# S5 in a two-layer diffusion trunk: elementwise work on VectorE alone, with both directions in scan order

## The chip, the cores and the metric

The kernel runs on one core of one Trainium2 chip. A core has TensorE (PE in the profile) for matmuls, VectorE (DVE), ScalarE (ACT) and GpSimd (POOL) for elementwise work, SyncE (SP), which issues DMAs here, and 16 DMA engines. Each engine takes its instructions in the order of its own queue; an instruction whose operands are not ready holds up all that is queued behind it. The metric is the time of one execution on the device in microseconds. The median of three runs of the kernel before is 2175.32 us (2174.04 to 2178.39).

## What is computed

The reference is a trunk of two layers. In each, a modulated RMSNorm feeds one input projection and three token mixers side by side: an S5 state-space model, a bidirectional Mamba-2 (SSD) and windowed attention. Their outputs are merged through gates; then a second norm feeds an expert-choice mixture of 16 SwiGLU experts. There are 256 latent and 256 context tokens of width 1024. The change touches S5 only: 32 groups of 16 channels, each with 64 complex states, run once forward and once backward.

```python
def s5_scan(u, abr, abi, bbr, bbi, h0, reverse):
    if reverse:
        u = jnp.flip(u, 1)
    bur = jnp.einsum('gpk,bngk->bngp', bbr, u)
    bui = jnp.einsum('gpk,bngk->bngp', bbi, u)
    ...   # h[n] = a * h[n-1] + bu[n], complex, over the tokens

def s5_readout(hr, hi, c_re, c_im, reverse):
    y = (jnp.einsum('gkp,bngp->bngk', c_re.astype(F32), hr)
         - jnp.einsum('gkp,bngp->bngk', c_im.astype(F32), hi))
    return jnp.flip(y, 1) if reverse else y
```

The backward direction scans the context tokens in reverse and then the latent tokens in reverse. In layer 1 only latent tokens are needed at the output.

## The kernel before

The program runs mixing of layer 0 (0 to about 702 us), its experts (to 1188), mixing of layer 1 (to about 1680) and its experts (to the end). S5 is a generator, `s5_gen`, of eight batches a layer, four groups in each. The host function of the mixing calls one batch at four places in the SSD loop and one after each of four pairs of attention heads; the input projection (L122, L125, from split weights of L113) and the modulation matmuls (L165) fill TensorE in between. A scheduler that follows a model of times turns the program into one order for each engine; the pools of tiles set which instruction must wait for which.

Within a batch the 512 tokens are 64 chunks of 8. Steps and lines:

1. DMAs of ScalarE's queue load `bc` (B and C) and `Ub` (the input by chunk).
2. `bb`, the discretised B, three rows on VectorE and three on GpSimd (L614 to L619); ScalarE puts them into `bst` (L620, L621).
3. For each direction d, d = 0 on VectorE and d = 1 on GpSimd: `gp`, the input block of a chunk (L631 to L633, with `tmp`), and `cp9`, the output table (L637 to L639). `gp` is transposed on TensorE (L642) and evicted to `ti` by ScalarE (L643).
4. `pk` (L648): the in-chunk kernel. ScalarE and VectorE copy it into `kr` (L650 to L653), a part of the tile of `tmp`; a DMA stores it to `kd` in DRAM (L655) and four DMAs read it back as the Toeplitz tile `W` (L657).
5. The rotation table `er`, `ei` (L665 to L667, the real half on VectorE, the other on GpSimd).
6. `px` (L674): the input of every chunk. Eight products with the rotation on VectorE (L683 to L686), read from PSUM, two sums on GpSimd (L687, L688), eight scans of 64 columns on VectorE (L691), products for the rotation back (L696 to L699) and the shifted states `hs` (L706 to L709) on both engines.
7. `yp`: per group one matmul with `W` (L713) and two with `cp9` and `hs` (L715); then the GELU on ScalarE and VectorE and a store.

All four PSUM results (two transposes, pk, px, yp) take their bank from the tag `s5`, which has one buffer, so they follow each other in the order in which the program asks for them. The SBUF tiles (four of 128 x 2048, named rb) hold one batch and are used again by the next: a write into `tmp` waits until the store of `kr` to `kd` has read it.

## Time and profile before

| | us |
|---|---|
| median of three runs | 2175.32 (2174.04 to 2178.39) |
| span of the profiled execution | 2175.6 |
| TensorE busy | 1879.4 (86%) |
| VectorE busy | 1040.2 (48%) |
| GpSimd busy | 589.0 (27%) |
| ScalarE busy | 554.9 (26%) |

The busy shares are means over stages with different limits. In the expert stages the DMA engines move some 409 GB/s and TensorE waits for weights. In the mixing stages TensorE is close to full, and the other engines prepare what it reads. What S5 is worth is therefore read from the mixing stages, from the waits of TensorE and the order in which instructions stand there.

### The profile page before, as it was taken

The numbers are of one execution on the slowest core, as the hardware profiler recorded it, in microseconds if no ns is written. First come the engines' busy times: TensorE is split into PE (matmuls) and PEld (weight loads), VectorE is DVE, ScalarE is ACT, GpSimd is POOL, SyncE is SP. The second block draws the span as 40 slices with busy tenths as digits, with TensorE's granted clock in tenths as the row PEclk, the third lists the DMA queues.
The fourth block names the chain that finished last, engine by engine and source line by source line (L and its number), as shares of the span: only waits on it lengthen the run. The fifth ranks groups of instructions, "written<-read, shape, count | busy, mean of one in ns | idle before, by whom it ended". The sixth has DMA issues, their size and how long they took to land. (4 is left out here: it accounts for less than half of the span.)

```text
span 2175.6 us, 29618 instructions
## 1 busy us (share of the span) xinstructions
PE 1879.4 (86%) x11292; PEld 1127.1 (52%) x11292; DVE 1040.2 (48%) x2234; ACT 554.9 (26%) x1200; POOL 589.0 (27%) x644
## 2 busy tenths in 40 slices
PE   6899999999999997986897898989998997776675
PEld 4577777788787432322332576778897322111111
DVE  6888786663256227121123469788656222212122
ACT  4335644442343100000000433535443100000000
POOL 1645476542242002000003235486533000000000
PEclk9999989999998998998898998989998899999798
DMA  9464333336345998999999355343477899999997
GB/s 268 156 183 127 114 90 107 99 104 220 90 155 203 410 349 351 409 408 409 404 409 351 107 185 172 107 129 86 125 244 271 348 409 409 409 409 409 409 409 274
DMA packets 265310, 561.72 MB, mean 258 GB/s; under 512 B 44048, under 2 KB 132560, under 8 KB 264912
## 3 DMA queue, kind: packets, MB, share of 16 engines
q1 hardware_dynamic: 232864, 541.83, 68.0%
q10 hardware_dynamic: 32304, 18.00, 3.0%
q8 instruction: 89, 1.46, 0.3%
q14 instruction: 53, 0.43, 0.1%
HBM read 552.00 MB, written 7.77 MB: 257 GB/s over the span
## 5 line engine op out<-in xcount | busy, mean ns | idle before, releaser
L122 PE MATMUL bk_mm<-hh,wh 128*128 128x512 f32 (+1 forms) x704 | 254.2, 375 | 12.5 <-ACT xp L800 6.7
L122 PE MATMUL bk_mm<-hl,wh 128*128 128x512 f32 (+1 forms) x704 | 247.6, 365 | 0.0
L113 POOL TENSOR_TENSOR wl<-w,wh 128x1024 fp32r<-128x1024 f32 x64 | 157.0, 2452 | 223.5 <-ACT wh L110 171.1
L110 ACT ACTIVATE wh<-w 128x1024 fp32r<-128x1024 f32 x140 | 147.9, 1058 | 215.9 <-PE bk_mm L122 106.6
L125 PE MATMUL bk_mm<-hh,wl 128*128 128x512 f32 (+1 forms) x704 | 163.0, 361 | 1.5 <-POOL wl L113 1.5
L122 PEld LDWEIGHTS bk_mm<-hh,wh 128*128 128x128 f32 x704 | 139.6, 199 | 36.1 <-ACT xp L800 8.2
L122 PEld LDWEIGHTS bk_mm<-hl,wh 128*128 128x128 f32 x704 | 139.6, 199 | 17.7 <-issue 1.4
L113 DVE TENSOR_TENSOR wl<-w,wh 128x1024 fp32r<-128x1024 f32 x76 | 99.8, 1315 | 72.6 <-ACT wh L110 32.4
L125 PEld LDWEIGHTS bk_mm<-hh,wl 128*128 128x128 f32 x704 | 119.6, 195 | 20.0 <-POOL wl L113 1.7
L1389 PE MATMUL bk_mm<-rb,xeT 128*64 128x512 f32 x512 | 122.1, 601 | 3.3 <-DMA rb<-w_e_up 2.0
L1419 PE MATMUL bk_mm<-xw,xeT 128*32 128x512 f32 x448 | 107.3, 628 | 16.5 <-DMA xw<-w_e_gate 11.4
L1424 DVE SCALAR_TENSOR_TENSOR hd<-fth,bk_mm 64x512 f32<-64x512 f32 x16 | 10.9, 681 | 208.4 <-ACT fth L1422 208.4
L1441 DVE SCALAR_TENSOR_TENSOR YE<-bk_mm,grow 32x512 f32<-32x512 f32 x64 | 44.0, 687 | 129.6 <-PE bk_mm L1436 115.8
L1422 ACT ACTIVATE fth<-bk_mm 64x512 f32<-64x512 f32 x16 | 9.4, 590 | 377.7 <-PE bk_mm L1419 377.7
L1389 PE MATMUL bk_mm<-xw,xeT 128*64 128x512 f32 x320 | 82.1, 613 | 13.5 <-DMA xw<-w_e_gate 13.5
L603 POOL MEMSET rb<- 128x256 f32 x2 | 1.2, 588 | 319.0 <-PE bk_mm L1389 305.0
L1393 DVE SCALAR_TENSOR_TENSOR fth<-fth,bk_mm 128x512 f32<-128x512 f32 x16 | 11.0, 687 | 157.3 <-ACT fth L1392 157.3
L1389 PEld LDWEIGHTS bk_mm<-rb,xeT 128*64 128x64 f32 x512 | 40.1, 139 | 78.6 <-issue 69.8
L1409 DVE SCALAR_TENSOR_TENSOR YE<-bk_mm,grow 32x512 f32<-32x512 f32 x64 | 44.0, 687 | 73.3 <-PE bk_mm L1405 56.5
L1419 PE MATMUL bk_mm<-rb,xeT 128*32 128x512 f32 x304 | 68.0, 603 | 8.3 <-DMA rb<-w_e_up 6.1
L1366 PE MATMUL bk_ps<-YE,Gt 128*128 128x512 f32 x128 | 61.7, 612 | 11.9 <-DVE YE L1441 9.1
L1419 PEld LDWEIGHTS bk_mm<-xw,xeT 128*32 128x32 f32 x448 | 24.1, 114 | 88.7 <-issue 55.5
(560 smaller groups left out, 3883.5 us busy)
## 6 DMA issues: line engine op xcount, KB each, us to landing
xw<-w_e_gate SPq DMA_DIRECT2D x67, 1024.0 KB, 11.5
rb<-w_e_up SPq DMA_DIRECT2D x59, 1024.0 KB, 17.4
xw<-w_e_down SPq DMA_DIRECT2D x54, 1024.0 KB, 14.0
w<-w_in SPq DMA_DIRECT2D x92, 512.0 KB, 4.7
rb<-w_e_gate SPq DMA_DIRECT2D x43, 1024.0 KB, 16.6
w<-w_mod SPq DMA_DIRECT2D x80, 512.0 KB, 4.1
xw<-w_e_up SPq DMA_DIRECT2D x29, 1024.0 KB, 14.0
w<-w_e_down SPq DMA_DIRECT2D x46, 512.0 KB, 14.0
```

Source lines behind the costliest of these rows:

```text
L110: S.activation(r(hi), raw, AF.Copy)
L113: e.tensor_tensor(r(lo), raw, hi, op=OP.subtract)
L122: PE.matmul(ps, wh(m, k), xv, start=first and k == 0 and i == 0, stop=False)
L125: PE.matmul(ps, wl(m, k), xs[k](m)[0], start=False, stop=last and k == n - 1)
L1366: PE.matmul(ps, Gt[:, tt - tts[0], e // ne, :], YE[:, tt // 2 if full else 0, n, :], start=True, stop=True)
L1389: PE.matmul(ps[64 * n:64 * n + 64, :], xeT[:, k, e, :], w[:, n * 512:n * 512 + 512], start=k == 0, stop=k == 7)
L1393: V.scalar_tensor_tensor(th, th, 1.0, pg, op0=OP.add, op1=OP.mult)
L1409: V.scalar_tensor_tensor(YE[q0:q0 + 32, si, n, :], py[o:o + 32, :], 0.5, g2[o:o + 32, si, n * 512:n * 512 + 512], op0=OP.mult, op1=OP.mult)
L1419: PE.matmul(pg[o:o + 32, :], xeT[:, k, e, :], w[:, n * 512:n * 512 + 512], start=k == 0, stop=k == 7)
L1422: S.activation(th[:64], pg[:64], AF.Tanh, scale=0.5)
L1424: V.scalar_tensor_tensor(hd[64:128], th[:64], 1.0, pg[:64], op0=OP.add, op1=OP.mult)
L1441: V.scalar_tensor_tensor(YE[q0:q0 + 32, 0, n, :], py[o:o + 32, :], 0.5, g2[o:o + 32, 1, n * 512:n * 512 + 512], op0=OP.mult, op1=OP.mult)
```

## The change

- All elementwise work of S5 stands on VectorE; GpSimd keeps three fills at the start of a layer.
- Both directions are kept in scan order. The direction d = 1 is mirrored by the matmuls of px and yp, which read `Ub` and `hs` with a negative step; the rotation needs no mirrored views.
- px is laid out by real and imaginary part first, so that one row of 512 columns turns both parts of all groups (L659), two rows of 256 make the sums (L660, L661), and one scan of 512 columns (L662) does all eight sequences. Its factor `rho` is written out to 512 columns with a zero at the start of each sequence, by two ScalarE copies (L614).
- The tables `Aa` and `Ab` have 9 columns in place of 10. `cp9` is made for all nine places in five rows (L665, L670, L671); the ScalarE copies into it (L626) are gone.
- px is asked for ahead of pk, so the `s5` bank goes transposes, px, pk, yp. `er`, `ei` (L654 to L656), the rotation (L659 to L661), the scan and `cp9` stand ahead of `pk` (L676), `kr` (L678 to L681), the store to `kd` (L683) and the loads of `W` (L685). The rotation back (L692, in layer 1 L696), `hs` (L701, L702) and `yp` (L706, L709) follow.

The diff, without most of the removed lines, which are printed above:

```diff
-        Aa = keep("aa", 640).rearrange("p (q i) -> p q i", i=10)
-        Ab = keep("ab", 640).rearrange("p (q i) -> p q i", i=10)
-        G.memset(Aa, 0.0)
-        G.memset(Ab, 0.0)
+        Aa = keep("aa", 576).rearrange("p (q i) -> p q i", i=9)
+        Ab = keep("ab", 576).rearrange("p (q i) -> p q i", i=9)
...
-                    ov = ov[:, :, :, 1:10] if d == 0 else ov[:, :, :, 0:9]
...
-            xr, xi = sl(4, 64), sl(4, 64)
+            rho = sl(8, 64)
-            kr = tmp.rearrange("p a b -> p (a b)")[:, 784:1024]
-            pq = ti.rearrange("p a b -> p (a b)").rearrange("p (i t c) -> p i t c", i=4, t=4)
+            flat = lambda v: v.rearrange("p a b -> p (a b)")
+            kr = flat(tmp)[:, 784:1024]
+            xx = flat(gp)[:, :512].rearrange("p (r t) -> p r t", r=2)
+            PQ = flat(ti).rearrange("p (i r t) -> p i r t", i=2, r=2)
+            mir = lambda v: v.rearrange("p (s c) -> p s c", s=2)[:, :, ::-1]
+            G.memset(rho, 0.0)
...
+                for ri in range(2):
+                    S.activation(rho[:, 4 * ri:4 * ri + 4, 1:64], sp["rho"][:, q4, None].to_broadcast([128, 4, 63]), AF.Copy)
+                ft = flat(tmp)
+                for i, nm in enumerate(("fr", "fi")):
+                    V.tensor_tensor(ft[:, 256 * i:256 * i + 256].rearrange("p (r t k) -> p r t k", r=2, k=16), bc[:, 0:2],
+                                    sp[nm][:, None, g8, None].to_broadcast([128, 2, 8, 16]), op=OP.mult)
+                fb = bb.rearrange("p r t k -> p r (t k)")
+                V.tensor_tensor(fb[:, 0], ft[:, 0:128], ft[:, 384:512], op=OP.subtract)
+                V.tensor_tensor(fb[:, 1], ft[:, 128:256], ft[:, 256:384], op=OP.add)
                 S.activation(bst[0:64, :, 0:16], bb[0:64, 0], AF.Copy)
...
                 for d in range(2):
+                    for dst, r_, tb in ((gp, 0, A_), (tmp, 1, B_)):
+                        V.tensor_tensor(dst[:, td].rearrange("p t (k s) -> p t k s", s=8),
+                                        bb[:, r_, td, :, None].to_broadcast(sh),
+                                        tb[:, td, None, d:d + 8].to_broadcast(sh), op=OP.mult)
+                V.tensor_tensor(flat(gp), flat(gp), flat(tmp), op=OP.add)
+                for d in range(2):
                     pt = bank("s5")
                     for j in range(4):
                         PE.transpose(pt[:, j * 128:j * 128 + 128], gp[:, 4 * d + j], ident)
+                    S.activation(ti[:, 4 * d:4 * d + 4].rearrange("p t n -> p (t n)"), pt, AF.Copy)
+                px = bank("s5")
+                pxv = px.rearrange("p (r t c) -> p r t c", r=2, t=4)
+                for d in range(2):
+                    for j in range(4):
+                        g2 = j % 2
+                        uv = Ub[:, j, :] if d == 0 else mir(Ub[:, j, :])
+                        for ri in range(2):
+                            o = pxv[64 * g2:64 * g2 + 64, ri, 2 * d + j // 2, :]
+                            PE.matmul(o if d == 0 else o.rearrange("p (s c) -> p s c", s=2),
+                                      ti[:, 4 * d + j, 64 * ri:64 * ri + 64], uv, start=True, stop=True)
...
+                for i, (dst, x0, x1, op) in enumerate(((er, "E8r", "E8i", OP.subtract), (ei, "E8i", "E8r", OP.add))):
+                    dv = dst.rearrange("p t (m i) -> p t m i", i=8)
+                    tv = xt[:, i].rearrange("p t (m i) -> p t m i", i=8)
+                    V.tensor_tensor(dv, E8[x0], F8["F8r"], op=OP.mult)
+                    V.tensor_tensor(tv, E8[x1], F8["F8i"], op=OP.mult)
+                    V.tensor_tensor(dv, dv, tv, op=op)
+                turn_ = [flat(v)[:, None, :].to_broadcast([128, 2, 256]) for v in (er, ei)]
+                for i in range(2):
+                    V.tensor_tensor(PQ[:, i], px.rearrange("p (r t) -> p r t", r=2), turn_[i], op=OP.mult)
+                V.tensor_tensor(xx[:, 0], PQ[:, 0, 0], PQ[:, 1, 1], op=OP.add)
+                V.tensor_tensor(xx[:, 1], PQ[:, 1, 0], PQ[:, 0, 1], op=OP.subtract)
+                V.tensor_tensor_scan(flat(gp)[:, :512], flat(rho), flat(gp)[:, :512], 0.0, OP.mult, OP.add)
+                sh = [128, 4, 9, 16]
+                ct = flat(tmp)
+                V.tensor_tensor(cp9, bc[:, 2, :, None, :].to_broadcast([128, 8, 9, 16]),
+                                A_[:, :, :, None].to_broadcast([128, 8, 9, 16]), op=OP.mult)
+                for d in range(2):
+                    td = slice(4 * d, 4 * d + 4)
+                    cv = ct[:, :576].rearrange("p (t i k) -> p t i k", i=9, k=16)
+                    V.tensor_tensor(cv, bc[:, 3, td, None, :].to_broadcast(sh), B_[:, td, :, None].to_broadcast(sh), op=OP.mult)
+                    V.tensor_tensor(cp9[:, td], cp9[:, td], cv, op=OP.add)
                 pk = bank("s5")
...
                 for j in range(4):
                     dma5(W[:, j, :], bass.AP(tensor=kd.tensor, offset=kd.offset + (b * 4 + j) * 32 * 240,
                                              ap=[[240, 16], [16, 8], [1, 128]]))
+                w_ = slice(0 if full else 31, 63)
+                x4 = xx.rearrange("p r (t c) -> p r t c", c=64)
+                P4 = PQ.rearrange("p i r (t c) -> p i r t c", c=64)
+                if full:
+                    for i in range(2):
+                        V.tensor_tensor(PQ[:, i], xx, turn_[i], op=OP.mult)
+                else:
+                    for i, v in enumerate((er, ei)):
                         for ri in range(2):
+                            V.tensor_tensor(P4[:, i, ri, :, w_], x4[:, ri, :, w_], v[:, :, w_], op=OP.mult)
+                for g2 in range(2):
+                    ir = slice(64 * g2, 64 * g2 + 64)
+                    pv = P4[ir].rearrange("p i r (d q) c -> p i r d q c", d=2)
+                    ov = hs.rearrange("p (q g) d c -> p g d q c", g=2)[:, g2][:, :, :, w_.start + 1:64]
+                    V.tensor_tensor(ov[0:64], pv[:, 0, 0, :, :, w_], pv[:, 1, 1, :, :, w_], op=OP.add)
+                    V.tensor_tensor(ov[64:128], pv[:, 0, 1, :, :, w_], pv[:, 1, 0, :, :, w_], op=OP.subtract)
                 yp = bank("s5")
                 for j in range(4):
                     o = yp[:, j * 64 + c_lo:j * 64 + 64]
                     PE.matmul(o, W[:, j, :], Ub[:, j, c_lo:], start=True, stop=False)
                     for d in range(2):
-                        PE.matmul(o, cp9[:, 4 * d + j, 1 - d:9 - d, :].rearrange("p i k -> p (i k)"), hs[:, j, d, c_lo:],
+                        hv_ = hs[:, j, 0, c_lo:] if d == 0 else mir(hs[:, j, 1, :])[:, c_lo // 32:]
+                        PE.matmul(o if d == 0 else o.rearrange("p (s c) -> p s c", c=32),
+                                  cp9[:, 4 * d + j, 1 - d:9 - d, :].rearrange("p i k -> p (i k)"), hv_,
                                   start=False, stop=d == 1)
```

Three places in the order of the engines' instructions. The first is TensorE in the fifth batch of layer 0, before: transposes (L642), pk (L648, into bank bk_s_3527), px (L674), W (L713); L165 is the modulation, L122 the projection, L973, L1033, L1037 and L169 belong to the neighbours.

```order
L642 MATMUL bk_s_3521<-kc,rb_1606 128x128 x4
...
L648 MATMUL bk_s_3527<-rb_1608,rb_1607 32x128 x8
L165 MATMUL bk_mm<-w,sil 32x128 x20
...
L674 MATMUL bk_s_3551<-rb_1608,rb_1606 64x64 x10
L973 MATMUL bk_ps<-dgr,kc 128x128 x2
L674 MATMUL bk_s_3551<-rb_1608,rb_1606 64x64 x6
...
L1037 MATMUL bk_ps<-vt,pT 128x64 x2
L713 MATMUL bk_s_3602<-rb_1608,rb_1607 128x64
L169 MATMUL bk_mm<-kc,cpart 128x128
```

And the same batch in the changed kernel: px is L646, pk L676, W L706, yp L709; L917, L958 and L125 belong to the neighbours.

```order
L646 MATMUL bk_s_3409<-rb_1606,rb_1604 64x64 x13
L917 MATMUL bk_ps<-qm,kc 128x256
L646 MATMUL bk_s_3409<-rb_1606,rb_1604 64x64 x3
...
L958 MATMUL bk_ps<-kc,zq 128x1 x12
L676 MATMUL bk_s_3442<-rb_1606,rb_1605 32x128 x7
L958 MATMUL bk_ps<-kc,zq 128x1 x4
L676 MATMUL bk_s_3442<-rb_1606,rb_1605 32x128
...
L125 MATMUL bk_mm<-hh,wl 128x512 x8
L165 MATMUL bk_mm<-w,sil 32x128 x10
L706 MATMUL bk_s_3466<-rb_1606,rb_1605 128x64
L709 MATMUL bk_s_3466<-rb_1607,rb_1606 128x64 x2
```

Between rows 713 and 720 of the second list, left out there, stand eight matmuls of L122 with 512 columns each. pk has moved behind px, and W follows pk with 16 matmuls of 512 columns and ten of L165 between, while px and more stood between before.

The next place is GpSimd, before, in the attention half of layer 0: a batch's input block (L631 to L633) behind the rotary rows (L925), its second factor `tmp` in L632, which waits for the store of the batch before it to `kd`.

```order
L631 TENSOR_TENSOR rb_1606<-rb_1607,sp_aa 128x512
L632 TENSOR_TENSOR rb_1607<-rb_1607,sp_ab 128x512
L633 TENSOR_TENSOR rb_1606<-rb_1606,rb_1607 128x512
L113 TENSOR_TENSOR wl<-w,wh 128x1024
L736 TENSOR_TENSOR yl<-y_1442,yh 128x512
L638 TENSOR_TENSOR rb_1607<-rb_1608,sp_ab 128x512
L736 TENSOR_TENSOR yl<-y_1442,yh 128x512 x2
L687 TENSOR_TENSOR rb_1609<-rb_1609 128x256
```

In the changed kernel none of these S5 rows is on GpSimd; there is VectorE, in the sixth batch: the rotation back (L692), `hs` (L701, L702), then the next batch's block (L629), the `kr` rows (L680, L681) and the write into `tmp` (the second L629). L1008 and L1034 are attention's row maximum and eviction, L113 a weight split.

```order
L692 TENSOR_TENSOR rb_1604<-rb_1604,rb_1607 128x512 x2
L1041 RECIPROCAL sm<-sm 128x8
L701 TENSOR_TENSOR rb_1607<-rb_1604 64x2x2x63
L702 TENSOR_TENSOR rb_1607<-rb_1604 64x2x2x63
...
L629 TENSOR_TENSOR rb_1604<-rb_1605,sp_aa 128x512
L654 TENSOR_TENSOR rb_1607<-sp_e8i,sp_f8r 128x256
...
L680 TENSOR_TENSOR rb_1605<-rb_1605,bk_s_3702 128x16
L1011 SCALAR_TENSOR_TENSOR nm<-mx,nsink 128x2
L681 SCALAR_TENSOR_TENSOR rb_1605<-kc,cl,rb_1605 128x16
L113 TENSOR_TENSOR wl<-w,wh 128x1024
L629 TENSOR_TENSOR rb_1605<-rb_1605,sp_ab 128x512
```

The write into `tmp` that waits for `kd` has moved from GpSimd to VectorE, close behind the rows that fill `kr`, and the `kr` rows stand behind `hs`.

## Rows read from the trace of the kernel before

**Rows 1.** Stretches: length, then busy us (count) of each engine, PEclk, DMA, GB/s.

```profile
54.00:216.00 162.00, 144.09 (x1159) 106.55 (x1148) 138.64 (x291) 68.68 (x164) 89.94 (x122) 0.95 0.50 155
216.00:324.00 108.00, 104.68 (x807) 79.50 (x810) 84.13 (x169) 54.62 (x141) 64.83 (x65) 0.95 0.36 104
324.00:486.00 162.00, 161.75 (x1156) 127.51 (x1148) 107.31 (x262) 72.82 (x173) 86.88 (x95) 0.99 0.37 104
486.00:648.00 162.00, 161.62 (x707) 128.28 (x705) 60.66 (x65) 55.53 (x73) 56.51 (x32) 1.00 0.48 151
...
1242.00:1404.00 162.00, 144.78 (x1251) 113.39 (x1249) 124.16 (x238) 65.44 (x158) 69.54 (x82) 0.92 0.53 160
1404.00:1586.00 182.00, 166.91 (x1398) 147.08 (x1397) 137.01 (x305) 76.94 (x173) 113.69 (x123) 0.93 0.41 113
```

**Rows 2.** Waits of PE: line waited for, us in total, times, longest us.

```profile
PE bk_mm L122 <- ACT xp L800: 6.7, 5, 3.5
...
PE bk_s L648 <- ACT rb L643: 3.0, 2, 2.7
PE bk_s L715 <- DVE rb L706: 3.0, 4, 1.5
...
PE bk_s L674 <- DVE rb L652: 2.3, 2, 1.4
...
PE bk_s L713 <- DMA rb<-kd: 2.0, 2, 1.3
...
PE bk_s L715 <- POOL rb L706: 1.4, 2, 0.7
...
PE bk_s L715 <- POOL rb L709: 0.5, 1, 0.5
```

**Rows 3.** Groups of VectorE, 54 to 1590 us: busy us, mean ns, idle before.

```profile
L691 DVE TENSOR_TENSOR_SCAN rb<-sp_rho,rb 128x64 f32<-128x64 f32 x128 | 45.1, 415 | 5.6 <-POOL rb L687 5.6
...
L631 DVE TENSOR_TENSOR rb<-rb,sp_aa 128x512 f32<-128x512 f32 x16 | 15.4, 965 | 0.2
...
L698 DVE SCALAR_TENSOR_TENSOR rb<-rb 128x132 f32<-128x132 f32 x8 | 2.6, 319 | 0.0
```

**Rows 4.** The same of GpSimd: the costliest and the last S5 group.

```profile
L639 POOL TENSOR_TENSOR rb<-rb,rb 128x512 f32<-128x512 f32 x16 | 24.7, 1541 | 1.1
...
L697 POOL TENSOR_TENSOR rb<-rb 128x132 f32<-128x132 f32 x8 | 4.8, 601 | 8.9 <-DVE rb L691 7.5 <-DVE yt L1039 1.4
```

**Rows 5.** Single lines: duration in ns, least, median and most; first and last start.

```profile
L631 DVE TENSOR_TENSOR rb<-rb,sp_aa x16: 675/684/2650, 90.6 to 1524.5; 128x512 f32<-128x512 f32 x16
...
L683 DVE TENSOR_TENSOR rb<-bk_s,rb x32: 273/281/292, 143.2 to 1570.0; 128x128 f32<-128x128 f32 x32
...
L113 DVE TENSOR_TENSOR wl<-w,wh x76: 1209/1224/2161, 35.7 to 1658.9; 128x1024 fp32r<-128x1024 f32 x76
...
L665 DVE TENSOR_TENSOR rb<-sp_e8r,sp_f8r x16: 411/426/965, 82.5 to 1561.7; 128x256 f32<-128x256 f32 x16
...
L691 DVE TENSOR_TENSOR_SCAN rb<-sp_rho,rb x128: 256/260/2418, 149.5 to 1575.2; 128x64 f32<-128x64 f32 x128
...
L455 DVE TENSOR_TENSOR_SCAN cum<-kc,selm x3: 672/678/679, 678.7 to 1679.8; 32x256 f32<-32x256 f32 x3
...
L650 ACT ACTIVATE rb<-bk_s x16: 254/259/283, 125.7 to 1565.3; 128x128 f32<-128x128 f32 x16
```

**Rows 6.** The store to kd, L655: who waited for it, and its landing.

```profile
  POOL rb L632: 39.8, 8
...
DMA to landing us min/median/max: 1.7/3.4/5.4
```

**Rows 7.** The loads of W, L657: from issue to landing.

```profile
DMA to landing us min/median/max: 2.1/2.4/4.4
```

**Rows 8.** Two stretches around a wait of PE near 158 us, as in Rows 1.

```profile
150.00:158.50 8.50, 6.44 (x60) 4.37 (x51) 8.33 (x21) 2.28 (x4) 6.62 (x9) 1.00 0.58 185
158.80:165.70 6.90, 6.90 (x27) 5.51 (x26) 6.90 (x10) 2.19 (x5) 3.90 (x5) 0.51 0.68 205
```

80 lines of the change are left out of this document (5 added, 75 removed).

## The prediction, made before the changed kernel was run

> **What bounds the kernel now.** I read the table of stretches first, because an average over the span mixes five different programs. In the first layer's mixing TensorE is busy 144.1 of 162 us, then 104.7 of 108, then 161.75 of 162 and 161.6 of 162 [rows 1]; from 216 us on nothing that is done for S5 can make that layer shorter, except by opening a hole. In the second layer it is 144.8 of 162 and 166.9 of 182 [rows 1], so there some 32 us of idle time lie in the stretches where S5 runs, and 18 us lie in the first stretch of layer 0. VectorE is at 138.6 of 162 us in that first stretch and between 107 and 137 us in the others [rows 1]: full, but not the limit. The expert stages are fed by DMA; S5 does not run there, and the change touches none of their instructions.
>
> Second, the waits of TensorE. Those that S5 causes are six kinds of row: 3.0 + 3.0 + 2.3 + 2.0 + 1.4 + 0.5, or 12.2 us in all [rows 2]. That is the whole that S5 itself can give back, out of 2175.6. The same view lists as much again that is not S5's but hangs on VectorE or ScalarE, the convolution's L800 with 6.7 us at its head [rows 2].
>
> Third, the costs of the work itself. S5 has two elementwise streams. On VectorE 25 groups of rows, from the scans of 45.1 us down to 2.6 us, add to 273 us, or 17.1 us for each of the sixteen batches [rows 3]. On GpSimd 22 groups, from 24.7 to 4.8 us, add to 281 us, or 17.6 us a batch [rows 4].
>
> **The change part by part.**
>
> *GpSimd's share goes.* 281 us leave GpSimd. TensorE waits for GpSimd's S5 rows 1.4 + 0.5 us [rows 2], so the removal itself is worth under 2 us. It can pay in another way: VectorE's S5 rows are stretched. L631 takes 0.684 us at the median and 0.965 in the mean, up to 2.65 [rows 3, 5]; L683, which reads one operand from PSUM, takes 0.273 to 0.292 us in all 32 of its runs [rows 5]. So rows with two operands in SBUF are held up, and beside GpSimd's rows is the likeliest place; these others are not.
>
> *VectorE's new sum.* For one batch in layer 0, by widths: the B terms are two rows of 256 columns at 0.426 (L665) and two of 128 at 0.281 (L683), 1.40; the block inputs four of 512 at 0.684 (L631) and one of 1024 at 1.224 (L113), 3.96; the rotation table six of 256 at 0.42, 2.52; rotation two of 512, 1.37; sums two of 256, 0.84; the output tables one of 1152, scaled from the 1024, and four of 576, scaled from the 512, 4.36; the rotation back 1.37; the hs rows four of 252, 1.68 [rows 5]. The scan: L691 takes 0.260 us for 64 columns and L455 0.678 for 256, a slope of 2.2 ns a column, so 512 columns take about 1.24 us [rows 5]; eight of the old ones took 8 x 0.260 = 2.08 clean, and 45.1/16 = 2.8 as traced [rows 3]. The sum is 18.7 us, in layer 1 (narrower rotation back) about 17.9. Against 17.1 us as traced VectorE gets 1.6 us more in a batch of layer 0, against its own clean time (12.8 by the same medians) 6. So GpSimd's 281 us of work cost VectorE some 20 us net: it does it at half the price and is no longer held up. VectorE's total hardly moves, and I cost it at nothing.
>
> *The old S5 waits* are edges between S5 steps (L642 to L648, L652 to L674, L706 to L715). All those edges are re-ordered; I take the full 12 us away and book what comes in their place below. Bounds: 0 and 12.
>
> *Relief of other waits.* Without GpSimd's S5 rows the non-S5 rows of VectorE get shorter too. TensorE is idle for those in layer 1 and before 216 us only. The rows that could profit hold some 15 us (the 6.7 us of L800 and the shorter ones that follow it). I take 5 us off, bounds 0 and 15.
>
> *The round trip through DRAM comes last.* This is the step that I think decides. One PSUM bank is shared by the transposes, pk, px and yp. Before, pk stood ahead of px: ScalarE and VectorE copied it into kr, kr went to kd in DRAM and came back as W while px, the rotation, the scan and the rotation back ran. Now px is ahead of pk, and the trip starts when the rotation has read px. Its length: two copies of 0.26 (L650), two VectorE rows of 16 columns (under the 0.28 of L683 with 128; 0.2 taken), the kd store 3.4 us from issue to landing, the first W load 2.4 us: 6.7 us [rows 5 to 7]. The order of TensorE's instructions in the fifth batch leaves between the last pk and the first W matmul 16 matmuls of 512 columns and ten small ones of L165. In a stretch without idle time 707 matmuls took 161.6 us, 0.229 each [rows 1]; 16 of them and ten quarters are 4.2 us. So TensorE waits 6.7 - 4.2 = 2.5 us, if VectorE takes the kr rows at once. It does not: they stand behind rotation, sums, scan, rotation back, the hs rows and two rows of the next batch, 7.6 us by the prices above, from the end of px; pk ends about 2.5 us behind px, and that makes the wait up to 5 us longer, some 8 us at most. Four batches are as short as this (4.3 us or less, the second, fourth, fifth and thirteenth); the other twelve have 6.5 to 15 us. Four times 2.5 to 8 is 10 to 32 us, middle about 20. Bounds for all: 2 us (the 2.0 that the same wait has now [rows 2]) and 32. I take +20, since the kr rows' place on VectorE is fixed by the order.
> The Trainium skill would make this term smaller: DMA: Bandwidth & Descriptors, section Anatomy of one DMA — SWDGE (gpsimd) path, gives a fixed cost of about 2.0 us for a DMA, so an estimate for two in series is 4.0 us and not 5.8, and the sum would come out some 7 us lower, at 2177. The kd and W rows of this trace, 3.4 and 2.4 us, are the measured ones, and the sum goes by them.
>
> *VectorE waits where GpSimd waited.* kr lies in the tile tmp, and the next batch's write to tmp has to wait until kd has read it. That wait is now GpSimd's, 39.8 us in eight times [rows 6], and costs nothing there. In the new order the same write (L629) is VectorE's, one to eight rows behind L681. In the sixth batch one row of 1.22 us lies between, so VectorE stands 3.4 - 1.2 = 2.2 us; times 16 is 35 us of VectorE. Queued behind it are the row maxima and evictions of attention, for which TensorE's next matmuls wait. VectorE has 23 to 55 us of air in each stretch [rows 1]; I take +3, bounds 0 and 35.
>
> *The clock.* After the wait of TensorE that ends near 158 us the granted clock is 0.51, the 1.2 GHz level, for 6.9 us, where it had been 1.00 [rows 8]. Half of such a stretch is lost, some 3.5 us. Eight microseconds more of waits than before are about one more such stretch: +3, bounds -5 and +10.
>
> The rest has one answer each: the two rho copies and the dropped copies of L626 on ScalarE are about even, matmul counts do not change, and the mirrored reads I cost at nothing for want of a row (bounds 0 and 2).
>
> **Sum.** 2175.6 - 12 - 5 + 20 + 3 + 3 = 2184.6 us of span. The median of the runs is 0.3 below the profiled span, so **2184 us**.
>
> **The rivals.**
> *Faster.* Relief is at its upper end and the trip is mostly covered: the hold-up that L631 shows is lifted from every VectorE row of the mixing that reads two operands in SBUF, the weight splits and the convolution too, and with a shorter VectorE queue the kr rows come early. For it: L631's mean is 1.4 times its median [rows 3, 5]. Against: 324 to 648 us has no idle time at all to give. -12 - 15 + 10 = -17, so 2158. A page of the Trainium skill speaks for this case (SBUF — State Buffer, section Who interferes with whom): a VectorE instruction with two SBUF inputs contends with a GpSimd instruction that reads SBUF, and the one that comes second is blocked until the other has ended; by it nearly all of this stretching would go with GpSimd's rows, and this trace's L631 and L683 agree with the rule.
> *No change.* The trip is covered by other matmuls in nearly all batches, as now (2.0 us): -12 - 5 + 10 + 3 + 3 = -1, so 2175. For it: the trip costs TensorE no more than that in the trace, and twelve of the sixteen batches have cover for its 6.7 us.
> *Much slower.* VectorE's stand at tmp reaches TensorE each time: 35 in place of 3, so 2216; it decides from the point where the rows between L681 and L629 hold under 3.4 us while TensorE's next matmul needs a VectorE row behind them. Against: in several batches small rows lie between, and TensorE has slack in layer 1.
>
> **How the numbers follow.** Forecast 0.40 (its own range 2175 to 2194), faster 0.30, no change 0.18, much slower 0.12. A measurement of this kernel tells about 0.2%, 4.4 us, from no change. Faster by more: all of the faster rival and a little of the no-change case, 0.33; within: 0.22; slower: 0.45. The range has to hold most of the faster rival, down to its bound (-12 - 15 + 2 = -25, 2150), and stops short of the much slower one: 2150 to 2207.
>
> **What would show it.** Right: TensorE's waits list the W matmul behind kd or behind the kr rows with 15 us or more, and S5's other waits are gone; GpSimd's S5 rows are absent; VectorE's 512-column rows have mean equal to median; the one scan takes 1.2 us; L629 waits for kd on VectorE. Wrong: a W wait of under 5 us (no change or faster); a TensorE busy time in 324 to 486 us that falls by more than 20 us (much slower); a rise of the granted clock in layer 1 with fewer idle spots (faster).

## The result, and the profile of the changed kernel

The changed kernel is slower: 2198.38 us at the median (2190.29 to 2208.98, four runs) against 2176.86 (2174.04 to 2179.96), a ratio of 1.0106 with a 95% interval of 1.0069 to 1.0142. The prediction said slower, 2184, with 2150 to 2207 as its range; the side is right, and the measured loss of 21.5 us is two and a half times the forecast one. The profiled execution has a span of 2198.2 us, 22.6 more than before. Everything below that is read from a trace is read from one execution of its kernel; the four runs of the changed kernel lie 19 us apart.

The stages that answer to [rows 1], in the same columns, of the changed kernel:

```profile
54.00:216.00 162.00, 144.69 (x1089) 106.02 (x1089) 133.75 (x281) 68.34 (x161) 39.63 (x63) 0.93 0.47 147
216.00:324.00 108.00, 104.16 (x859) 81.18 (x856) 94.36 (x153) 56.98 (x147) 27.57 (x20) 0.96 0.37 112
324.00:486.00 162.00, 160.48 (x1104) 126.50 (x1104) 110.15 (x229) 66.26 (x155) 33.42 (x21) 0.96 0.39 118
486.00:648.00 162.00, 159.37 (x690) 125.32 (x688) 57.26 (x69) 54.77 (x78) 50.91 (x30) 0.98 0.40 124
...
1242.00:1404.00 162.00, 142.09 (x1247) 112.97 (x1246) 117.75 (x221) 61.23 (x145) 27.96 (x28) 0.93 0.52 157
1404.00:1586.00 182.00, 168.16 (x1326) 147.11 (x1327) 146.65 (x289) 82.81 (x188) 46.94 (x35) 0.89 0.38 106
```

GpSimd's column has halved or better in the stretches with S5 (from 486 us on in layer 0 there is almost none). TensorE's column has moved by under 3 us, and VectorE's by some 3 to 10 us, up in three stretches and down in three. What has moved against the kernel is the last column but two: the granted clock is 0.96 and 0.98 from 324 to 648 us, where it was 0.99 and 1.00, and 0.89 from 1404 us where it was 0.93.

Whole stages say it more plainly. The two mixing stages, from 54 us (layer 1: from the last expert matmul of layer 0) to the first expert matmul; first two lines before, then two of the changed kernel:

```profile
54.00:698.60 644.60, 618.10 (x4056) 481.68 (x4044) 428.41 (x888) 269.79 (x587) 312.14 (x322) 0.97 0.45 138
1184.80:1686.80 502.00, 450.39 (x3418) 371.80 (x3414) 350.70 (x710) 204.48 (x446) 238.17 (x244) 0.92 0.51 158
```
```profile
54.00:710.90 656.90, 625.80 (x4035) 488.16 (x4033) 438.94 (x836) 270.69 (x585) 170.70 (x144) 0.95 0.43 135
1198.80:1708.10 509.30, 451.23 (x3418) 374.71 (x3414) 367.76 (x701) 206.58 (x446) 118.91 (x94) 0.91 0.51 157
```

Layer 0 is 12.3 us longer, layer 1 some 7, and the experts take the rest. VectorE is busy 10.5 and 17 us longer, 28 in all, for 261 us that GpSimd no longer works in these stages.

The waits of TensorE, changed kernel (line waited for, us in total, times, longest):

```profile
PE bk_mm L165 <- DMA w<-w_mod: 9.0, 6, 3.4
PE bk_s L706 <- DMA rb<-kd: 8.1, 7, 2.6
...
PE bk_ps L968 <- DVE dgr L967: 7.4, 2, 6.9
...
PE bk_ps L875 <- DVE wt L864: 4.7, 3, 2.5
...
PE bk_s L706 <- DVE rb L632: 2.5, 1, 2.5
...
PE bk_ps L845 <- DVE BC L811: 1.8, 1, 1.8
...
PE bk_s L676 <- DVE rb L659: 0.8, 1, 0.8
...
PE bk_s L709 <- DVE rb L701: 0.4, 1, 0.4
```

W waits for kd 8.1 us, where it waited 2.0 [rows 2]; S5's waits for its own elementwise steps fell from 10.2 to 4.7 us; and the waits of the other work in the mixing (projection, convolution, SSD, attention, gates), all their rows added, rose from 41.9 to 53.4. L968, L875 and L845 are SSD rows that wait for VectorE. Of the 11.5 us by which the other waits rose, 5.8 are for VectorE, 4.3 for ScalarE and 3.0 for DMAs, and the rest fell by 1.6.

The wait for kd by layers, first the mixing of layer 0, then that of layer 1:

```profile
PE bk_s L706 <- DMA rb<-kd: 1.0, 1, 1.0
```
```profile
PE bk_s L706 <- DMA rb<-kd: 7.1, 6, 2.6
```

So most of the waiting for the round trip lies in layer 1, and most of the loss in layer 0.

The clock around a wait, changed kernel, as in [rows 8]:

```profile
316.00:326.00 10.00, 9.94 (x53) 8.19 (x54) 9.55 (x28) 2.25 (x7) 3.87 (x4) 0.66 0.17 61
326.00:331.00 5.00, 3.48 (x36) 2.45 (x34) 4.15 (x13) 0.00 (x0) 0.00 (x0) 1.00 0.54 156
331.00:342.00 11.00, 11.00 (x75) 8.34 (x76) 6.53 (x12) 3.63 (x10) 1.95 (x2) 0.55 0.20 62
342.00:352.00 10.00, 10.00 (x49) 7.70 (x49) 10.00 (x12) 6.32 (x14) 7.86 (x5) 0.98 0.65 204
```

From 326 to 331 us lies the fifth batch's W: TensorE stands 1.0 us before it, for kd, and 0.5 us a little later, for VectorE's L967. For the 11 us after that it works without a gap at a mean clock of 0.55, nearly all at the 1.2 GHz level; some 5 us are lost there. But the 0.66 of the first line shows that the clock had been low once already, ahead of W's hole:

```profile
298.60:314.90 16.30, 16.30 (x96) 13.14 (x97) 16.18 (x17) 7.06 (x13) 13.83 (x10) 1.00 0.34 105
314.90:320.40 5.50, 5.44 (x49) 4.90 (x48) 5.47 (x9) 1.34 (x3) 4.89 (x5) 0.82 0.33 95
318.40:325.20 6.80, 6.80 (x21) 5.44 (x22) 6.61 (x21) 1.64 (x6) 1.55 (x2) 0.50 0.00 0
```
```profile
314.94 2.73 PE L958 MATMUL bk_ps<-kc,zq 128*128 128x1 f32 x24
```

From 298.6 to 325.2 us TensorE stands for 0.06 us in all, and yet from 318.4 us it is at the 1.2 GHz level for 6.8 us. What it did just before were matmuls of one column (L958, part of the SSD's norm) and pk. So a slow stretch need not have a hole ahead of it.

**An account of the mixing time.** For each kernel below I took TensorE's time in the mixing stages of its profiled execution apart: its length, the time without a matmul (idle), and the length times one minus the granted clock, added up over slices of 3 us (clock). What is left is the work at full clock; the few matmuls whose records are missing count as idle in all of them. (Layer 1 is taken here from the exact end of layer 0's last expert matmul, so the changed kernel's length is 508.8 and not the 509.3 of the line above.)

| kernel | layer 0: length, idle, clock, left | layer 1: length, idle, clock, left | ratio of the runs to before |
|---|---|---|---|
| before | 644.6, 26.5, 22.4, 595.7 | 502.0, 51.6, 41.0, 409.3 | 1 |
| changed | 656.9, 31.1, 32.4, 593.4 | 508.8, 58.1, 46.2, 404.5 | 1.0106 (1.0069 to 1.0142) |
| e1, pk first | 646.8, 37.9, 16.1, 592.9 | 500.6, 51.5, 42.1, 407.0 | 1.0045 (1.0031 to 1.0060) |
| e2, kr in xt | 664.1, 39.5, 34.1, 590.5 | 507.3, 55.6, 48.9, 402.8 | 1.0109 (1.0096 to 1.0122) |
| e3, W elsewhere | 644.7, 30.1, 19.1, 595.6 | 520.2, 58.5, 62.1, 399.5 | 1.0087 (1.0073 to 1.0101) |
| e4, cp9 on GpSimd | 673.2, 44.0, 33.3, 595.8 | 505.2, 58.3, 44.4, 402.5 | 1.0161 (1.0143 to 1.0178) |
| b1, before, pk late | 660.6, 40.9, 31.2, 588.6 | 508.3, 58.0, 47.7, 402.5 | 1.0160 (1.0130 to 1.0190) |
| b2, before, VectorE alone | 675.7, 48.9, 34.1, 592.7 | 518.2, 56.7, 57.7, 403.8 | 1.0246 (1.0227 to 1.0266) |
| e5, e1, table three times | 681.1, 53.1, 41.4, 586.6 | 523.6, 62.0, 62.2, 399.4 | 1.0285 (1.0264 to 1.0305) |
| e6, e1, splits on GpSimd | 653.5, 35.6, 19.9, 598.0 | 512.0, 57.0, 47.8, 407.3 | 1.0140 (1.0113 to 1.0166) |
| e7, e1, table on GpSimd | 671.0, 37.7, 36.0, 597.3 | 503.1, 53.0, 45.0, 405.1 | 1.0140 (1.0115 to 1.0165) |
| e8, e7, kr in gp | 671.7, 44.3, 30.0, 597.5 | 510.2, 59.6, 45.2, 405.4 | 1.0192 (1.0169 to 1.0215) |
| e9, e1, no table | 647.2, 32.0, 19.3, 595.9 | 490.5, 48.2, 37.0, 405.3 | 0.9990 (0.9972 to 1.0007) |
| b3, before, wide scan | 667.5, 43.8, 30.9, 592.8 | 513.7, 57.8, 52.0, 403.9 | 1.0166 (1.0139 to 1.0193) |

The column "left" is the same within 12 us in 595 and 10 in 405, whatever the kernel. Idle time inside a slow stretch is taken off twice in it; taken off once, the work left is 593 to 602 and 412 to 418 us. So what made these kernels differ is where TensorE stood and at which clock it went on. How the loss splits between the two is less sure than their sum: e7 and e8 have nearly the same order in layer 0 and the same length within 0.7 us, and yet 6.6 us more idle and 6.0 us less clock loss. From before to the changed kernel: idle +4.6 and +6.5, clock +10.0 and +5.2, left -2.3 and -4.8, in sum +19.2; the rest of the span adds 3.4.

### The profile page after: what moved, and what is told of

It reads as the page before. It is cut to its first block, busy times and chain, and to the rows that moved or that the text cites. A ratio compares the mean times of both kernels' runs of the same rounds, so it can differ in the third digit from the quotient of the medians.

```text
span 2198.2 us, 29107 instructions
## 1 busy us (share of the span) xinstructions
PE 1889.1 (86%) x11292; PEld 1138.4 (52%) x11292; DVE 1067.8 (49%) x2186; ACT 559.5 (25%) x1200; POOL 320.4 (15%) x306
## 5 line engine op out<-in xcount | busy, mean ns | idle before, releaser
L122 PE MATMUL bk_mm<-hh,wh 128*128 128x512 f32 (+1 forms) x704 | 252.8, 373 | 12.4 <-ACT wh L110 5.6
L122 PE MATMUL bk_mm<-hl,wh 128*128 128x512 f32 (+1 forms) x704 | 246.6, 364 | 0.5 <-POOL hl L526 0.5
L113 POOL TENSOR_TENSOR wl<-w,wh 128x1024 fp32r<-128x1024 f32 x64 | 164.3, 2567 | 467.7 <-ACT wh L110 275.1
L125 PE MATMUL bk_mm<-hh,wl 128*128 128x512 f32 (+1 forms) x704 | 162.3, 362 | 0.6 <-DVE wl L113 0.6
L122 PEld LDWEIGHTS bk_mm<-hh,wh 128*128 128x128 f32 x704 | 140.0, 199 | 36.6 <-ACT wh L110 6.8
L122 PEld LDWEIGHTS bk_mm<-hl,wh 128*128 128x128 f32 x704 | 139.7, 199 | 18.4 <-POOL hl L526 0.9
L113 DVE TENSOR_TENSOR wl<-w,wh 128x1024 fp32r<-128x1024 f32 x76 | 98.9, 1302 | 64.1 <-ACT wh L110 23.7
L125 PEld LDWEIGHTS bk_mm<-hh,wl 128*128 128x128 f32 x704 | 119.9, 197 | 18.9 <-issue 1.2
L1414 PE MATMUL bk_mm<-xw,xeT 128*32 128x512 f32 x448 | 105.2, 617 | 20.5 <-DMA xw<-w_e_gate 12.3
L165 PE MATMUL bk_mm<-w,sil 128*32 128x128 f32 x1280 | 58.0, 288 | 11.0 <-DMA w<-w_mod 9.0
## 6 DMA issues: line engine op xcount, KB each, us to landing
w<-w_in SPq DMA_DIRECT2D x92, 512.0 KB, 4.5
w<-w_mod SPq DMA_DIRECT2D x80, 512.0 KB, 3.9
w<-w_e_down SPq DMA_DIRECT2D x46, 512.0 KB, 13.9
```

The source lines that it names most:

```text
L113: e.tensor_tensor(r(lo), raw, hi, op=OP.subtract)
L122: PE.matmul(ps, wh(m, k), xv, start=first and k == 0 and i == 0, stop=False)
L125: PE.matmul(ps, wl(m, k), xs[k](m)[0], start=False, stop=last and k == n - 1)
L165: PE.matmul(ps[32 * j:32 * j + 32, :128], sil[:, 2 * u + i, :], w[:, i, j * 128:j * 128 + 128], start=u == 0 and i == 0, stop=u == 3 and i ...
L1414: PE.matmul(pg[o:o + 32, :], xeT[:, k, e, :], w[:, n * 512:n * 512 + 512], start=k == 0, stop=k == 7)
```

## The experiments

Theory A: the loss is the round trip pk, kr, kd, W, which starts behind px. Theory B: it is VectorE's queue, in which rows of SSD and attention stand behind S5's. Theory C, formed on the way: neither quantity as such, but the order of the queues that each edit brings, through the holes in TensorE and the clock behind them.

One thing limits all that follows. The scheduler makes a new order for every edit, so hardly any experiment varies one thing alone. e2 moves one tile and e3 changes the source of one load; still TensorE's instructions stand in the changed kernel's order only for the first 739 and 492 of the program, to about 116 and 80 us. Only e8 keeps an order, that of e7 in layer 0.

### e1: the round trip ahead of px again

The 24 lines from `cp9` to the W loads are moved, unchanged:

```diff
+                V.tensor_tensor(cp9, bc[:, 2, :, None, :].to_broadcast([128, 8, 9, 16]),
...
+                pk = bank("s5")
...
                 px = bank("s5")
...
                 V.tensor_tensor_scan(flat(gp)[:, :512], flat(rho), flat(gp)[:, :512], 0.0, OP.mult, OP.add)
...
-                V.tensor_tensor(cp9, bc[:, 2, :, None, :].to_broadcast([128, 8, 9, 16]),
...
-                pk = bank("s5")
```

> The changed kernel with cp9, pk, kr, the kd store and the W loads moved ahead of px, as they stood before; all work still on VectorE. Theory A (the loss is the round trip pk, kr, kd, W, which now starts behind px): TensorE's waits at W for kd, 8.1 us in the changed kernel with 2.6 at most, fall under 3 us, the half-clock stretches behind them go, and the time comes back to 2180 to 2186. Theory B (the loss is VectorE's queue: rows of SSD and attention stand behind S5's rows, L811, L864 and L967 with some 14 us of waits): the W waits go but the time stays at 2192 to 2204, since cp9's 4.4 us a batch stand in VectorE's queue all the same.

Measured: 2185.42 us (2179.02 to 2191.25), ratio 1.0045. About 13 of the 21 us come back. TensorE's S5 waits of e1 (the profiled execution, 2179.8 us, is at the low end of its runs):

```profile
PE bk_s L709 <- DVE rb L701: 9.7, 3, 5.7
...
PE bk_s L670 <- DVE rb L655: 3.6, 1, 3.6
PE bk_s L636 <- ACT rb L637: 3.5, 2, 2.8
...
PE bk_s L706 <- DMA rb<-kd: 0.5, 1, 0.5
```

The time is what theory A forecast, and the wait for kd is gone. But the S5 waits that take its place, for `hs` (L701), are longer than it was, and TensorE's idle time is the same: 89.2 us in the changed kernel, 89.4 in e1. What came back is the clock, 78.6 to 58.2 us, and 16.3 of these 20.4 us lie in layer 0, where kd had held TensorE for 1.0 us. So the number fits theory A and the way to it does not.

### e2: kr out of the way of the next batch

```diff
-            kr = flat(tmp)[:, 784:1024]
+            kr = xt.rearrange("p i t c -> p (i t c)")[:, 0:240]
```

> The changed kernel with kr in the tile xt, which nothing of the next batch writes before the W loads have landed, in place of the end of tmp. VectorE's second L629 then no longer waits for the kd store. Theory A and theory B with the stand at kd as a part of it: L629's waits, 7.7 us in 7 times, go to 0, and the time falls by 0 to 8 us. If the stand at kd were the main cost (the prediction's much slower rival): 2180 or less. If it costs nothing: within 4 us of the changed kernel's 2198.

Measured: 2201.07 us, ratio 1.0109: nothing gained, as forecast for a stand that costs nothing. VectorE's wait of 7.7 us at L629 is gone from the trace; with the order changed besides, this does not measure its price by itself.

### e3: no round trip for W

```diff
-                    dma5(W[:, j, :], bass.AP(tensor=kd.tensor, offset=kd.offset + (b * 4 + j) * 32 * 240,
+                    dma5(W[:, j, :], bass.AP(tensor=ud.tensor, offset=ud.offset + (b * 4 + j) * 32 * 240,
```

> The changed kernel with the W tile loaded from the input block in DRAM, which lies there before the first batch, in place of kd (same shape and steps, so the W term of the output is left out in effect); kr is still made and stored. No W matmul waits for the round trip. Theory A: the whole price of the trip goes, 8.1 us of TensorE's waits (12.8 with the weight loads') and the clock behind them: 2178 to 2186. Theory B: the time stays within 6 us of 2198.

Measured: 2196.96 us, ratio 1.0087, which is theory B's forecast; theory A fails. No W waits for kd any more. By layers: layer 0's mixing is 644.7 us, that of the kernel before to 0.1 us, and shorter by 12.2 us than in the changed kernel, where kd had held TensorE for 1.0. Layer 1's is 520.2, 11 longer than in the changed kernel, with 62.1 us lost to the clock, though this is where 7.1 us of waits for kd went. TensorE's waits for S5's VectorE rows went from 4.3 to 12.4 us.

### e4: cp9 on GpSimd

The five rows of L665, L670 and L671 on GpSimd:

```diff
-                V.tensor_tensor(cp9, bc[:, 2, :, None, :].to_broadcast([128, 8, 9, 16]),
+                G.tensor_tensor(cp9, bc[:, 2, :, None, :].to_broadcast([128, 8, 9, 16]),
```

> The changed kernel with the five rows of cp9 (L665, L670, L671) on GpSimd in place of VectorE: 4.4 us of a batch leave VectorE's queue, about 70 us in all, GpSimd gets some 8 us a batch and stands beside VectorE again. Theory B: waits at L811, L864 and L967 shrink and the time falls to 2180 to 2190. Theory A: no gain, or a loss, since cp9 lies ahead of pk and is slower on GpSimd: 2195 to 2210.

Measured: 2211.55 us, ratio 1.0161, 1.6 us above theory A's range. cp9 stands ahead of pk and is slower on GpSimd, and W waits for kd longer. First GpSimd's rows, then TensorE's wait:

```profile
L671 POOL TENSOR_TENSOR rb<-rb,rb 128x576 f32<-128x576 f32 x32 | 50.3, 1571 | 1.8
```
```profile
PE bk_s L706 <- DMA rb<-kd: 14.1, 6, 4.5
```

The 14.1 us are 7.0 in layer 0 and 7.1 in layer 1. Layer 0 is 28.6 us over the kernel before, layer 1 only 3.2. Against the changed kernel layer 1 is 3.6 us shorter: that much, at most, is what theory B gets here.

### b1: the kernel before, with the round trip late

The block from `pk` to the W loads is moved, unchanged, behind the scans:

```diff
-                pk = bank("s5")
...
                 px = bank("s5")
...
                         V.tensor_tensor_scan(v[:, t_, :], sp["rho"][:, 4 * b + t_:4 * b + t_ + 1].to_broadcast([128, 64]),
                                              v[:, t_, :], 0.0, OP.mult, OP.add)
+                pk = bank("s5")
...
                 j0 = 0 if full else 31
```

> The kernel before, on both engines, with nothing changed but that pk, kr, the kd store and the W loads stand behind px, its rotation and the scans, as in the changed kernel. Theory A (the place of the round trip costs layer 0 some 10 us and the rest of the change little): 2184 to 2192, with W waiting for kd 8 us or more. If the trip costs only together with VectorE's longer queue (theory B): within 5 us of 2176.

Measured: 2207.42 us, ratio 1.0160. On the old kernel, with both engines at work, this edit alone costs more than the whole change, and more than either theory forecast. Its TensorE waits:

```profile
PE bk_mm L122 <- ACT xp L800: 10.3, 6, 3.4
PE bk_s L713 <- DMA rb<-kd: 7.3, 3, 3.4
PE bk_ps L973 <- DVE dgr L972: 6.7, 1, 6.7
```

W's wait for kd is 7.3 us, near the 8.1 of the changed kernel, and all of it lies in layer 1, whose mixing is 6 us longer than before. Layer 0 is 16 us longer, and there the list of TensorE's waits names neither kd nor a step of S5 (a weight load waits 0.5 us). So the edit is dear, but in layer 0 the waiting for the trip is not the price.

### b2: the kernel before, all of S5 on VectorE

```diff
-                    e = V if d == 0 else G
+                    e = V
...
-                        e = V if g2 == 0 else G
+                        e = V
```

and `V` for `G` in the other elementwise rows of the batch.

> The kernel before in its own order and its own instructions, with every elementwise row of S5 on VectorE: pk ahead of px, eight scans of 64, half-width rows. VectorE gets the 281 us of GpSimd's rows at its own price, about 140 us (9 a batch); the changed kernel's wide rows save some 4 us a batch of that. Theory B (VectorE's queue is what is left when the trip is back in its place): slower than e1 by VectorE's extra 60 us times a small share, 2188 to 2205. Theory A: near e1, 2180 to 2188.

Measured: 2226.47 us, ratio 1.0246, slower than either theory forecast. e1, with the trip in the same place, has 1.0045: the wide rows, the single scan and the order that came with them are worth some 2% on VectorE. They do not get it from VectorE's time alone: it is busy 449 + 371 us in b2's mixing stages and 444 + 359 in e1's, 16 us less, for some 43 us.

### e5: the price of VectorE's time, upward

The loop that makes `er` and `ei` stands three times in e1:

```diff
+                for i, (dst, x0, x1, op) in enumerate(((er, "E8r", "E8i", OP.subtract), (ei, "E8i", "E8r", OP.add))):
...
+                    V.tensor_tensor(dv, dv, tv, op=op)
```

> e1 (pk ahead of px) with the rotation table computed three times in place of once: 12 more rows of 256 columns, 5 us a batch, 80 us in all, on VectorE, for the same result. This is the price of VectorE's time. Theory B: a tenth to a third of it comes through, 2193 to 2210. Theory A: under 5 us, 2180 to 2190.

Measured: 2234.45 us, ratio 1.0285, the slowest of all and above both forecasts. The added rows cost 49 us against e1, spread over both layers. Their durations add to some 80 us, but VectorE's busy time in the mixing rose by 51 us only (803.7 to 854.3): durations of neighbouring rows overlap (in e1's mixing they add to 880 us), and some other rows got shorter. By that measure the price is about one to one.

### e9: the price of VectorE's time, downward

```diff
-                for i, (dst, x0, x1, op) in enumerate(((er, "E8r", "E8i", OP.subtract), (ei, "E8i", "E8r", OP.add))):
+                for i, (dst, x0, x1, op) in enumerate(((er, "E8r", "E8i", OP.subtract), (ei, "E8i", "E8r", OP.add)) if b == 0 else ()):
```

> e1 with the rotation table made for the first batch of a layer only and left out for the other seven (the output of S5 is then not the reference's): 14 times 2.5, or 35 us, leave VectorE and no engine takes them. Theory B: 0.6 of it comes back, 2160 to 2170. Theory C: 2178 to 2188. Against e7 it tells what GpSimd's rows beside VectorE cost.

Measured: 2172.18 us, ratio 0.9990 (0.9972 to 1.0007). It lies between the two forecasts. 35 us less give 13 us against e1: 10 in layer 1's mixing by the account above, none in layer 0's, where TensorE has little idle time to give, and the rest outside the mixing.

### e7 and e8: the table on GpSimd

```diff
-                    V.tensor_tensor(dv, E8[x0], F8["F8r"], op=OP.mult)
+                    G.tensor_tensor(dv, E8[x0], F8["F8r"], op=OP.mult)
```

and so for the other two rows of the loop; e8 has `kr = flat(gp)[:, 784:1024]` besides.

> e1 (pk ahead of px) with the rotation table er, ei on GpSimd: six rows of 256 columns, 2.5 us a batch, 40 us in all leave VectorE; GpSimd takes 0.63 to 0.8 us for each. Tripling the table cost 49 us for 80, so VectorE's time is worth about 0.6 us a us there. Theory B (that price holds downward too): 2160 to 2172, under the kernel before. Theory C (the price is only on the upper side, or the two engines' hold-ups eat it): 2178 to 2190.

> e7 with kr in the second half of gp in place of the end of tmp: the next batch's first writes to gp and tmp then need not wait for the kd store, only the third does, one row or two later. VectorE stood 13.4 us in ten times at kd in e1. If VectorE's stand there costs at VectorE's price (0.6): 3 to 8 us under e7. If it is idle time that VectorE has anyway: within 4 us of e7.

Measured: e7 2206.93 us, ratio 1.0140; e8 2216.20, ratio 1.0192. Both are slower than e1 and outside every forecast. VectorE never waits for the table in e7's trace. But three groups of VectorE's S5 rows with two operands in SBUF are stretched more. First e7, then e1 (busy us, mean ns, idle before):

```profile
L646 DVE TENSOR_TENSOR rb<-rb,rb 128x576 f32<-128x576 f32 x32 | 31.2, 976 | 0.2
L645 DVE TENSOR_TENSOR rb<-rb,sp_ab 128x576 f32<-128x576 f32 x32 | 30.9, 967 | 0.1
L629 DVE TENSOR_TENSOR rb<-rb,sp_aa 128x512 f32<-128x512 f32 x32 | 28.6, 898 | 4.6 <-PE bk_s L636 4.2
```
```profile
L646 DVE TENSOR_TENSOR rb<-rb,rb 128x576 f32<-128x576 f32 x32 | 30.4, 952 | 0.2
...
L645 DVE TENSOR_TENSOR rb<-rb,sp_ab 128x576 f32<-128x576 f32 x32 | 26.7, 835 | 0.1
L629 DVE TENSOR_TENSOR rb<-rb,sp_aa 128x512 f32<-128x512 f32 x32 | 22.6, 710 | 1.2 <-PE bk_s L636 0.7
```

These three groups alone take 11 us more. Of the 40 us that left VectorE only 13 show in its busy time: 804 us in e1's two stages, 791 in e7's. That explains a gain that stayed out, not a loss of 21 us. The loss is in layer 0 (24 us), and of it 20 are clock at the same idle time (37.9 and 37.7 us): TensorE stands elsewhere.

e8 is 9 us slower than e7. In layer 0 the order is that of e7, but for the two writes of L629, which change places, and a few more rows; there it takes the same time. VectorE's stand at kd is the same there too (8.9 and 9.0 us): the write that waits is now the other one, and the edit took nothing away. In layer 1 the order differs, and there it takes 7 us more. Layer 0's mixing of e7, then of e8:

```profile
54.00:725.00 671.00, 633.33 (x4034) 492.61 (x4032) 430.27 (x788) 269.93 (x585) 209.59 (x192) 0.95 0.43 132
54.00:725.70 671.70, 627.40 (x4035) 488.04 (x4033) 432.92 (x788) 269.72 (x585) 212.50 (x193) 0.96 0.42 132
```

### e6: weight splits for the idle GpSimd

```diff
-    turn = ["VG"]
+    turn = ["VGG"]
```

and in the two later settings of `turn` one G more, on e1.

> e1 with more of the weight splits (L113) on the now idle GpSimd: two of three in place of one of two, in layer 1's gates one of two in place of one of three. Some 24 rows of 1.22 us leave VectorE, GpSimd takes 2.4 us for each. Theory B: 2172 to 2182, at or under the kernel before. If GpSimd's slower rows come late instead: 2186 to 2196 with waits of TensorE for L113 on GpSimd.

Measured: 2201.45 us, ratio 1.0140. GpSimd made 76 splits from 54 to 1640 us at 2.49 us each, VectorE 46. TensorE's waits for splits are small:

```profile
PE bk_mm L125 <- POOL wl L113: 2.9, 3, 1.5
PE bk_mm L125 <- DVE wl L113: 2.5, 1, 2.5
```

So neither forecast holds: the splits were hardly late, and the kernel is slower than e1 in both layers. Nor did VectorE get its relief. 24 splits with 30 us left it, but its busy time in the mixing fell by 2 us (803.7 to 801.6): its other rows got longer, with GpSimd busy 54 us more.

### b3: the kernel before with wide scans

```diff
-                for t_ in range(4):
-                    for v in (xr, xi):
-                        V.tensor_tensor_scan(v[:, t_, :], sp["rho"][:, 4 * b + t_:4 * b + t_ + 1].to_broadcast([128, 64]),
-                                             v[:, t_, :], 0.0, OP.mult, OP.add)
+                S.activation(rho[:, :, 1:64], sp["rho"][:, q4, None].to_broadcast([128, 4, 63]), AF.Copy)
+                S.activation(rho[:, :, 0:1], sp["rho"][:, q4, None], AF.Copy, scale=0.0)
...
+                for i in range(2):
+                    V.tensor_tensor_scan(xf[:, 256 * i:256 * i + 256], rf, xf[:, 256 * i:256 * i + 256], 0.0, OP.mult, OP.add)
```

`rho` lies in the first 256 columns of `gp`, which are free once the transposes have read them.

> The kernel before, both engines and its own order, with one part of the change alone: two scans of 256 columns over a written-out rho with a zero at each start, in place of eight scans of 64. VectorE's 45.1 us of scans become 32 x 0.68, or 22 us; ScalarE writes rho twice a batch. If taking time from VectorE and from S5's chain pays as it did for e9 (13 us for 35): 2162 to 2170, under both kernels. If the order that comes out decides (theory C): 2172 to 2186, either side of the kernel before, and the sum of TensorE's idle time and clock loss says which.

Measured: 2213.21 us, ratio 1.0166, far above both forecasts. At the median the scans take what was priced; in the mean they take 0.93 us, and VectorE's busy time in the mixing stays at 779 us:

```profile
L696 DVE TENSOR_TENSOR_SCAN rb<-rb,rb x32: 659/683/1772, 148.9 to 1610.4; 128x256 f32<-128x256 f32 x32
```

One thing that the edit moves besides is when `gp` is free. Before, VectorE's half of the next batch's `gp` is ready 26 to 43 us ahead of the last yp of the batch under way; in b3 3 to 14 us, since `rho` lies in that half until the scan (the first pair of layer 1 left out here). In the changed kernel, which keeps `xx` in `gp`, the block is ready only 2 to 12 us ahead, in one batch after it. In all of them the transposes start 2 to 14 us behind that yp, whose bank they share. Whether the shorter lead, or the order that came with it, is the cause of b3's 36 us I have not separated.

## Why the prediction was right, and where it was not

**The side holds; the reason given for it does not carry it.** The step that was to decide was the round trip behind px, with +20 us of TensorE's waits. Layer 0 does follow the trip's place: taking it away (e3) or putting it back ahead (e1) brings layer 0 from 656.9 to 644.7 and 646.8 us, and moving it in the kernel before (b1) makes layer 0 16 us longer. But the waits for it are not what costs there: kd holds TensorE 1.0 us in layer 0 of the changed kernel and never in b1's. And an edit that leaves the trip in its place lengthens layer 0 as much: b3 by 23 us against before, e7 by 24 against e1. In layer 1, where 7.1 of the 8.1 us are waited, e1 has 8 us less than the changed kernel and e3, without the trip, 11 more. So that the time came out on the forecast side is in part luck: the trip cost what the no-change rival had booked for it (10), and the loss came from two terms that were forecast at -5 and +3. Neither sign of the prediction was met: the W wait is neither 15 us or more nor under 5.

**The size of that term was wrong in its make-up.** It was put at +20 of waits. W waits 8.1 us for kd. In the fifth batch, which I had put at 2.5 to 8, TensorE stands 1.0 us before W: the matmuls in between were priced at full clock, and most of them ran at half. Of the four batches that were called short, the fifth alone waits for kd; the second stands 2.5 us at W for VectorE's L632, and the other two not at all. The other waits for kd are in batches that were called covered. The lengths of the two DMAs came out as a sum of 4.8 us, not 5.8, by their medians:

```profile
DMA to landing us min/median/max: 1.7/1.7/3.8
```
```profile
DMA to landing us min/median/max: 2.1/3.1/7.5
```

(the store to kd, L683, and the loads of W, L685, changed kernel). The estimate from the Trainium skill's figure (DMA: Bandwidth & Descriptors, section Anatomy of one DMA — SWDGE (gpsimd) path), two times 2.0, is about as far below that as the rows of before are above. The section gives it for DMAs that GpSimd issues; these are ScalarE's, so no run here tests it.

**The clock was the mis-sized term.** +3 was forecast; the account above gives +15.2, or 14.3 with idle time taken off once. I took the clock as an extra to the waits, in proportion to them. The runs show no such proportion: e1 and the changed kernel have the same idle time and 20 us of clock between them, and so have e1 and e7 in layer 0. And one slow stretch of the changed kernel has no hole ahead of it, only small matmuls.

**The relief had the wrong sign.** Other waits were to fall by 5 us; they rose by 11.5. The stretching went in part. SSD's L869 has 875 ns in the mean before and, as L864, 685 in the changed kernel. The scan has 1.23 us in the mean, as priced (1.24), and the 512-column rows that read PSUM are untouched, but several of S5's other rows are stretched still. GpSimd works 290 us in these stages, and the stretching is where it does: L629's 51 rows without a GpSimd instruction at the same time take 0.69 us, every one of them, and the 13 with one take 1.45 in the mean and up to 2.89. The same rows by groups:

```profile
L671 DVE TENSOR_TENSOR rb<-rb,rb 128x576 f32<-128x576 f32 x32 | 30.9, 966 | 0.1
...
L629 DVE TENSOR_TENSOR rb<-rb,sp_ab 128x512 f32<-128x512 f32 x32 | 27.0, 850 | 7.8 <-DMA kd<-rb 7.7
...
L659 DVE TENSOR_TENSOR rb<-bk_s,rb 128x512 f32<-128x512 f32 x32 | 20.6, 684 | 7.0 <-PE bk_s L646 6.9
L662 DVE TENSOR_TENSOR_SCAN rb<-rb,rb 128x512 f32<-128x512 f32 x16 | 19.7, 1233 | 0.2
```

So "mean equal to median" holds for L659 and the scan, nearly for L692 (0.71 against 0.68), and not for L629 (0.85 against 0.69). The rule that stood beside the faster rival, in the Trainium skill (SBUF — State Buffer, section Who interferes with whom), agrees with these rows: L659 reads one operand from PSUM and is not stretched, L629 and L671 read both from SBUF. L665 reads both from SBUF too, and four of its rows with GpSimd beside them are not stretched (1.36 us, as the others); why, no run shows. The stretching did not decide the time: L864 got shorter, and TensorE waited longer for it (4.7 us against 1.8). That SSD's rows wait because S5's second half stands in the same queue is my reading of it; no run shows it by itself, and only half of the 11.5 us are waits for VectorE.

**VectorE's total, costed at nothing,** was forecast 20 us longer and is 28, and busy time there is not free: e5 pays 49 us for 51 more, e9 gets 13 for 35 less. Neither price may be read as a constant, as e7 shows.

**VectorE's stand at kd, +3,** was there (7.7 us in seven times, 39.8 on GpSimd before [rows 6]), and without it the kernel is no faster (e2). The much slower rival falls with it.

**The old S5 waits, -12,** went by half, from 10.2 to 4.7 us without kd; the sum of all S5 waits is 12.8 against 12.5.

The sum of +9 was thus about right in the waits, +11 of idle time by the account, for wrong reasons, and short by the clock. What stays open is the cause: which part of the order of the changed kernel makes its holes and slow stretches, and whether the round trip, VectorE's longer queue or neither brought that order about. The 12 experiments gave eleven kernels slower than before by 0.4 to 2.9% and one level with it, also where work was only taken away or moved to an idle engine. b3 was expected within 2162 to 2186 us and e6 within 2172 to 2196; they took 2213 and 2201. That the kernel before lies at a favourable order, so that nearly any edit loses, is the rival that fits all of them; it is not shown. A run of the changed instructions in an order that is held fixed would test it, and there is none. No version here beats it; e9, which leaves work out, equals it.
